# Moving token loads, norms and block splits forward, and spreading transposes and a convolution over steps, in a hybrid mixer layer

## The chip, the cores and the metric

The kernel runs on one core of a Trainium2 chip. The metric is the device time of one execution in microseconds; the number given for a kernel is the median of several runs. One further execution was taken by the hardware profiler, and every row below comes from it.

## The reference, cut to what matters

One layer of a streaming encoder over 512 tokens of width 2048 and 256 memory tokens of the same width:

```python
h = rms_norm(x, norm_g)
proj = h @ w_in                       # 2048 -> 13312
(a_b, a_c, a_x, a_z, q, k, v, b_z, mq, m_z, g_a, g_b, g_m) = split(proj)
ya = (short_conv_mixer(a_b, a_c, a_x, conv_w) * silu(a_z)) @ w_branch_a
yb = (chunk_band_attention(q, k, v, ...) * silu(b_z)) @ w_branch_b
mk, mv = split(rms_norm(mem, mem_norm_g) @ w_mem_kv)
ym = (memory_attention(mq, mk, mv, ...) * silu(m_z)) @ w_branch_m
merged = sigmoid(g_a + b0) * ya + sigmoid(g_b + b1) * yb + sigmoid(g_m + b2) * ym
x = x + merged @ w_out
```

`short_conv_mixer` is `a_b * conv3(a_c * a_x)`, a causal convolution of three taps along the tokens, per channel. So `a_c * a_x` has to be turned (channels on partitions) before the taps, and `a_b * silu(a_z)` likewise before it multiplies the result.

## The kernel before, in words

The program is a list of **steps**. Each step has weight loads, subtractions of weights (`adds`), a split of a weight tile and its matmuls. `run_steps` (line 123) walks the list and emits, for step i, in this order: the loads of step i + 6, the adds of step i, the split of step i + 2, the matmuls of step i, its `post` (the evacuation of finished banks), whatever `at_step(i, ...)` put there, what `after(n, ...)` put there n steps earlier, and then the waiting `task`s as far as a budget of 1.35 per step goes. Every engine runs its own instructions in the order in which they were emitted (class `Engine`, line 40), so this order is the order of each queue. A function that stands later in a step stands behind everything of that step on each engine that it uses.

Steps 0 to 15 are the projection of memory (`kv_steps`, line 405): eight fp32 matmuls of 128x512 each, from a 512 KB weight load `raw_kv` and the turned memory `mT`. Beside them the tokens are made ready: 16 pieces of x of 256 KB are loaded (line 441), one token tile of 128 rows in four pieces; `x_norm(t)` (line 495) takes the squares of the four pieces on ScalarE, the reciprocal root on VectorE and GpSimd, and scales pieces 0 and 2 on VectorE, 1 and 3 on ScalarE; `x_turn(t, k4)` (line 503) turns one piece with four TensorE transposes, and VectorE evacuates it times the gain. `mem_piece` (line 349) does the same for memory.

From step 16 on the projection of the tokens runs in `pair`s of 28 steps (line 235), in the order q, k, v, cx, bz, mqz, az, then the gates. A pair multiplies two halves of the tokens with two column blocks of 512, in the seven-product scheme of Strassen and Winograd: products P1, P5, P6, P3, P7, P2, P4, four steps each. A step has 12 matmuls (two k tiles, two banks, three products of high and low parts). The left operands are the blocks A11, S1, S2, S4, S3, A12, A22 of the normalised tokens, made once: `H.do` (line 477) either combines two blocks with a VectorE operation on 128x1024 per half (s1 to s4), or splits one into a high part (a cast on ScalarE) and a low part (a subtraction on VectorE), also 128x1024 per half. The weights of each step are split in the same way (`split_w`, line 186: `whi` on ScalarE, `wlo` on VectorE; three buffers of each), and 16 of the 28 steps have a weight subtraction before them on VectorE.

Slots of SBUF are shared: S3 takes the slots of the raw memory, A22 high takes the slot of the combination S12, and S2 takes the slots of `mT`, so its low part can be written only after the last matmul of step 15.

The memory projection's results are rescaled by ScalarE (`post` in line 423) at the ends of steps 14 and 15; `heads_out` (line 364) then puts squares, a reciprocal root (`rstd`, over VectorE and GpSimd) and scaling of the keys among the tasks.

In the pair cx, the last product of a half multiplies two evacuated tiles (`go` in line 615) and turns the result (`u_turn`, line 598: four transposes per tile, two copies by ScalarE); both happen at the end of the same step, as tasks. After the last tile `conv` (line 589) runs as one task: for each of four channel groups one ScalarE multiplication and two VectorE operations over 512 tokens. In the pair az, `w_turn` (line 620) does for `a_b * silu(a_z)` what `u_turn` does for `a_c * a_x`.

Of the kernel before, what the change touches and what calls it, by code (L numbers as in the profile page):

```python
# [14 lines left out]
ALU = mybir.AluOpType  # L15
# [5 lines left out]
S = 512  # L21
# [44 lines left out]
def trunk_layer(ctx: ExitStack, tc, x, mem, gx, gm, w_in, w_kv, bg, cw, hg, relz, w_a, w_b, w_m, w_o, out):  # L66
    nc = tc.nc
    PE, ACT, DVE = Engine(tc, nc.tensor), Engine(tc, nc.scalar), Engine(tc, nc.vector)
    POOL, SP = Engine(tc, nc.gpsimd), Engine(tc, nc.sync)
# [17 lines left out]
    cw_sb = cst.tile([P, 3, 4], F32, name="cw_sb")  # L87
# [5 lines left out]
    def slot(i, name, shape=(P, 4, S), dtype=F32):  # L93
        return big.tile(list(shape), dtype, tag=f"s{i}", name=name)

    def cell(name, shape=(P, S)):
        return cel.tile(list(shape), F32, tag="c", name=name)

    def wide(name, shape=(P, 2, S), tag="pp"):
        return hds.tile(list(shape), F32, tag=tag, name=name)  # L100
# [8 lines left out]
    steps, later, todo, at = [], [], [], {}  # L109
# [3 lines left out]
    def after(n, fn):  # L113
        seq[0] += 1
        heapq.heappush(later, (clock[0] + n, seq[0], fn))

    def at_step(i, fn):
        at.setdefault(i, []).append(fn)

    def task(cost, fn):  # L120
        todo.append((cost, fn))
# [213 lines left out]
    def piece(dst, src, t, j):  # L335
        SP.dma_start(dst[:, j, :], src[t * P:(t + 1) * P, j * S:(j + 1) * S])
# [3 lines left out]
    xraw = [slot((13, 12, 3, 2)[t], f"x{t}") for t in range(NT)]  # L340
# [98 lines left out]
        steps[j - 1].loads.append(lambda j=j: first_loads(j))  # L439
    steps[2].loads.append(lambda: [SP.dma_start(d, s) for d, s in ((gx_sb, gx), (hg_sb, hg), (cw_sb, cw))])  # L440
    for i in range(16):
        steps[3 + i // 2].loads.append(lambda i=i: piece(xraw[i // 4], x, i // 4, i % 4))

    for k4 in range(4):
        at_step((-3, 0, 3, 5)[k4], lambda k4=k4: [mem_piece(t, k4) for t in range(NMT)])
# [49 lines left out]
    def x_norm(t):  # L495
        r = row_rstd(squares(xraw[t], f"x{t}"), f"x{t}")
        for j in range(4):
            if j % 2:
                ACT.mul(xraw[t][:, j, :], xraw[t][:, j, :], r)
            else:  # L500
                DVE.tensor_scalar_mul(xraw[t][:, j, :], xraw[t][:, j, :], r)

    def x_turn(t, k4):
        pt = bank(f"pt_x{t}_{k4}", (P, 4, P))
        for j in range(4):
            PE.transpose(pt[:, j, :], xraw[t][:, k4, j * P:(j + 1) * P], ident)
        DVE.tensor_tensor(H.f((k4 // 2, t // 2), k4 % 2)[:, :, (t % 2) * P:(t % 2 + 1) * P], pt,
                          gx_sb[:, 4 * k4:4 * k4 + 4].unsqueeze(2).broadcast_to([P, 4, P]), op=ALU.mult)

    for t in range(NT):  # L510
        b = 2 + 2 * t
        at_step(b, lambda t=t: x_norm(t))
        at_step(b + 1, lambda t=t: [x_turn(t, 0), x_turn(t, 1)])
        at_step(b + 2, lambda t=t: [x_turn(t, 2), x_turn(t, 3)])
    for i in range(2):
        for n, what in ((6 + i, "A11"), (8 + i, "A12"), (11, "s1"), (12, "s3"), (13, "S3"), (14, "S1"), (15, "s2"),
                        (16, "s4"), (17 + i, "S4"), (19 + i, "S2"), (22 + i, "A22")):
            at_step(n, lambda i=i, what=what: H.do(what, i))

    def w_pair(src, c0, c1=None):  # L520
# [15 lines left out]
    y_d = dram.tile([P, 4, S], F32, name="y_d")  # L536
# [18 lines left out]
    def silu(c, name):  # L555
        sg = cell(f"sg_{name}")
        ACT.activation(sg, c, AF.Sigmoid)
        DVE.tensor_mul(c, c, sg)
# [22 lines left out]
    kept, uT = {}, []  # L581

    def turned(c, name, put):
        pt = bank(f"pt_{name}", (P, 4, P))
        for j in range(4):
            PE.transpose(pt[:, j, :], c[:, j * P:(j + 1) * P], ident)
        put(pt)

    def conv():
        for j in range(4):  # L590
            u = uT[j // 2][:, j % 2, :]
            y = cell(f"cv{j}")
            ACT.mul(y, u, cw_sb[:, 2, j:j + 1])
            DVE.scalar_tensor_tensor(y[:, 1:], u[:, :S - 1], cw_sb[:, 1, j:j + 1], y[:, 1:], ALU.mult, ALU.add)
            DVE.scalar_tensor_tensor(y[:, 2:], u[:, :S - 2], cw_sb[:, 0, j:j + 1], y[:, 2:], ALU.mult, ALU.add)
            after(3, lambda j=j, y=y: SP.dma_start(y_d[:, j, :], y))

    def u_turn(t, c):
        if not uT:
            uT.extend(wide(f"uT{i}", tag=("pp", "qk")[i]) for i in range(2))  # L600

        def put(pt):
            for i in range(2):
                ACT.copy(uT[i][:, :, t * P:(t + 1) * P], pt[:, 2 * i:2 * i + 2, :])
        turned(c, f"u{t}", put)
        if t == NT - 1:
            task(1.5, conv)

    def cx_done(half, t0, cells):
        for i, c in enumerate(cells):  # L610
            t = t0 + i
            if half:
                kept["x", t] = c
            else:
                def go(t=t, c=c):
                    DVE.tensor_mul(c, c, kept["x", t])
                    task(0.8, lambda: u_turn(t, c))
                task(0.1, go)

    def w_turn(t, c):  # L620
        def put(pt):
            wt = cell(f"wt{t}", (P, 4, P))
            ACT.copy(wt, pt)
            after(2, lambda: SP.dma_start(wt_d[:, :, t * P:(t + 1) * P], wt))
        turned(c, f"w{t}", put)

    def bz_conv_done(half, t0, cells):
        for i, c in enumerate(cells):
            t = t0 + i
            if half:  # L630
                kept["z", t] = c
                task(0.7, lambda c=c: silu(c, "az"))
            else:
                def go(t=t, c=c):
                    DVE.tensor_mul(c, c, kept["z", t])
                    task(0.8, lambda: w_turn(t, c))
                task(0.1, go)

    pair("cx", H.left, w_pair(w_in, A_C, A_X), cx_done)
# [100 lines left out]
    for u in range(len(units)):  # L740
        i = n_g + EVERY * u
# [174 lines left out]
```

## Time and profile before

| | |
|---|---|
| median of 3 runs | 1528.65 us (1528.4 to 1529.83) |
| the profiled execution | 1527.54 us, its span 1525.8 us, granted TensorE clock 0.997 |
| TensorE busy (matmuls) | 1488.8 us, 98% of the span |
| weight loads of TensorE | 1201.5 us, 79% |
| VectorE busy | 1148.1 us, 75% |
| ScalarE busy | 707.0 us, 46% |
| chain that ended last | TensorE 87%, VectorE 8%, ScalarE 2%, issue 1%, DMA 1% |

The span runs from the first to the last instruction; the profiled time is 1.74 us longer than it. In the rows below PE is TensorE, DVE VectorE, ACT ScalarE, SP the queue that issues loads. In a row of the timeline the columns are start, duration (of the whole group), engine, line, operation, written tile and read tiles, shape, count, and in brackets the idle time before it with what ended it. All instructions carry line 48, a helper's, so tiles tell them apart.

### The profile page before, as it was taken

To read this page: it belongs to the slowest core of one execution; us is meant where nothing else is said; L and a number is where in the kernel's file an instruction comes from. 1 tells how busy PE (TensorE), PEld (TensorE's weight loads), DVE (VectorE), ACT (ScalarE), POOL (GpSimd) and SP (SyncE) were. 2 spreads that over 40 slices of the span, in tenths; PEclk is the share of its full clock that TensorE was granted. 3 is DMA by queue.
4 is the path that set the end of the run, shared out by engine and by line. 5 is a ranking of instruction groups with operands and counts; after the bars stand their busy time and mean duration, and the time that the engine had idled before them with its cause. 6 is when DMAs were issued, how large, how long until landed. Compare 5 with 4: busy or idle time off the path is not lost.

```text
span 1525.8 us, 17874 instructions
## 1 busy us (share of the span) xinstructions
PE 1488.8 (98%) x6696; PEld 1201.5 (79%) x6696; DVE 1148.1 (75%) x1393; ACT 707.0 (46%) x1102; POOL 22.0 (1%) x23
## 2 busy tenths in 40 slices
PE   8989999999899999999999999999999999998998
PEld 4568888788688888788888888888887888886787
DVE  3697778777788887787777878787887455579987
ACT  3665666543444455444444444444445343445442
POOL 0000000000000000000000000000000000000000
PEclk9999999999999999999999999999999999999999
DMA  9524354363426253525537263543736555510724
GB/s 331 180 69 149 126 169 141 99 214 110 138 64 212 65 179 91 186 88 190 169 117 257 90 214 104 176 166 97 254 138 232 193 194 188 204 43 21 248 83 131
DMA packets 139046, 233.45 MB, mean 153 GB/s; under 512 B 9808, under 2 KB 35408, under 8 KB 138320
## 3 DMA queue, kind: packets, MB, share of 16 engines
q1 hardware_dynamic: 130320, 215.54, 43.0%
q10 hardware_dynamic: 8640, 16.78, 3.3%
q8 instruction: 52, 0.85, 0.2%
q14 instruction: 34, 0.28, 0.1%
HBM read 198.73 MB, written 36.17 MB: 154 GB/s over the span
## 4 chain that ended last, share of the span: by engine, by line
PE 87%; DVE 8%; ACT 2%; issue 1%; DMA 1%; POOL 0%; SPq 0%; DVEq 0%; ACTq 0%; POOLq 0%
PE ps_wb L48 6%; PE psY_gb L48 4%; PE psY_ga L48 4%; PE ps_kv L48 3%; PE psY_gm L48 3%; PE psY_o L48 3%; PE psZ_gm L48 3%; PE psZ_gb L48 3%; PE psZ_ga L48 3%; PE ps_wa L48 3%; PE ps_wm L48 3%; PE psY_k L48 2%; PE psY_mqz L48 2%; PE psY_bz L48 2%; PE psY_az L48 2%; PE psY_cx L48 2%
## 5 line engine op out<-in xcount | busy, mean ns | idle before, releaser
L48 ACT CAST whi_o_P<-raw_o 128x1024 fp32r<-128x1024 f32 x56 | 58.7, 1054 | 85.7 <-DVE raw_o L48 21.0
L48 DVE TENSOR_TENSOR wlo_ga_P<-raw_ga,whi_ga_P 128x1024 fp32r<-128x1024 f32 x56 | 68.2, 1222 | 31.9 <-ACT whi_ga_P L48 31.4
L48 DVE TENSOR_TENSOR wlo_gb_P<-raw_gb,whi_gb_P 128x1024 fp32r<-128x1024 f32 x56 | 68.1, 1222 | 31.6 <-ACT whi_gb_P L48 31.5
L48 DVE TENSOR_TENSOR wlo_gm_P<-raw_gm,whi_gm_P 128x1024 fp32r<-128x1024 f32 x56 | 68.4, 1222 | 23.3 <-ACT whi_gm_P L48 23.3
L48 DVE TENSOR_TENSOR wlo_o_P<-raw_o,whi_o_P 128x1024 fp32r<-128x1024 f32 x56 | 68.2, 1221 | 20.1 <-ACT whi_o_P L48 19.9
L48 ACT CAST whi_gm_P<-raw_gm 128x1024 fp32r<-128x1024 f32 x56 | 58.7, 1051 | 20.9 <-PE psV_gm L48 4.8
L48 ACT ACTIVATE p<-p,nm 128x128 f32<-128x128 f32 (+3 forms) x32 | 18.0, 564 | 105.2 <-DVE nm L48 102.2
L48 ACT CAST whi_ga_P<-raw_ga 128x1024 fp32r<-128x1024 f32 x56 | 58.3, 1049 | 9.7 <-PE psY_az L48 3.3
L48 ACT CAST whi_gb_P<-raw_gb 128x1024 fp32r<-128x1024 f32 x56 | 58.4, 1049 | 6.9 <-PE psY_gb L48 2.3
L48 ACT COPY p<-ptp 128x256 f32<-128x256 f32 (+3 forms) x48 | 19.6, 408 | 89.4 <-PE ptp L48 89.4
L48 PE MATMUL ps_kv<-raw_kv,mT 128*128 128x512 f32 x128 | 58.1, 605 | 1.4 <-DMA raw_kv<-in_w_kv 1.4
L48 PE MATMUL ps_wb<-whi_wb,yb_hi 128*128 128x512 f32 x128 | 49.8, 389 | 0.0
L48 PE MATMUL ps_wb<-wlo_wb,yb_hi 128*128 128x512 f32 x128 | 49.8, 389 | 0.0
L48 PE MATMUL ps_wb<-whi_wb,yb_lo 128*128 128x512 f32 x128 | 49.8, 389 | 0.0
L48 ACT CAST whi_cx_P<-raw_cx 128x1024 fp32r<-128x1024 f32 x28 | 29.5, 1055 | 42.4 <-PE psY_cx L48 13.2
L48 DVE TENSOR_TENSOR wlo_cx_P<-raw_cx,whi_cx_P 128x1024 fp32r<-128x1024 f32 x28 | 34.3, 1223 | 18.9 <-ACT whi_cx_P L48 17.2
L48 PEld LDWEIGHTS ps_kv<-raw_kv,mT 128*128 128x128 f32 x128 | 24.2, 195 | 28.4 <-issue 26.4
L48 DVE TENSOR_TENSOR wlo_bz_P<-raw_bz,whi_bz_P 128x1024 fp32r<-128x1024 f32 x28 | 34.2, 1223 | 14.2 <-ACT whi_bz_P L48 14.1
L48 ACT CAST whi_bz_P<-raw_bz 128x1024 fp32r<-128x1024 f32 x28 | 29.5, 1052 | 33.4 <-PE psZ_bz L48 10.0
L48 DVE TENSOR_TENSOR wlo_mqz_P<-raw_mqz,whi_mqz_P 128x1024 fp32r<-128x1024 f32 x28 | 34.2, 1223 | 14.2 <-ACT whi_mqz_P L48 14.2
L48 DVE TENSOR_TENSOR wlo_v_P<-raw_v,whi_v_P 128x1024 fp32r<-128x1024 f32 x28 | 34.1, 1222 | 14.0 <-ACT whi_v_P L48 13.8
L48 ACT CAST whi_mqz_P<-raw_mqz 128x1024 fp32r<-128x1024 f32 x28 | 29.4, 1051 | 31.4 <-PE psZ_mqz L48 10.0
(661 smaller groups left out, 4676.5 us busy)
## 6 DMA issues: line engine op xcount, KB each, us to landing
raw_ga<-in_w_in SPq DMA_DIRECT2D x32, 512.0 KB, 4.7
raw_gb<-in_w_in SPq DMA_DIRECT2D x32, 512.0 KB, 5.2
raw_gm<-in_w_in SPq DMA_DIRECT2D x32, 512.0 KB, 5.2
raw_o<-in_w_o SPq DMA_DIRECT2D x32, 512.0 KB, 6.7
raw_kv<-in_w_kv SPq DMA_DIRECT2D x16, 512.0 KB, 7.7
raw_q<-in_w_in SPq DMA_DIRECT2D x16, 512.0 KB, 4.8
raw_k<-in_w_in SPq DMA_DIRECT2D x16, 512.0 KB, 4.8
raw_v<-in_w_in SPq DMA_DIRECT2D x16, 512.0 KB, 4.5
```

The source lines that it names most:

```text
L48: ins = getattr(self.engine, op)(*args, **kwargs)
```

## The change

The loads of x are attached two steps earlier (steps 1 to 8 in place of 3 to 10). `x_norm` is emitted at steps 1, 3, 4, 6 in place of 2, 4, 6, 8, with its transposes in the two steps after each. The block operations move forward by one to five steps and stand closer: the last, A22, at steps 17 and 18 in place of 22 and 23; s1 and s3 share step 9, s2 and s4 share step 12. `conv` becomes a function of one channel group, called 2, 4, 6 and 8 steps after the last `u_turn`. `u_turn` and `w_turn` are called one step after the multiplication (`after(1, ...)`) and not as tasks of the same step.

```diff
     for i in range(16):
-        steps[3 + i // 2].loads.append(lambda i=i: piece(xraw[i // 4], x, i // 4, i % 4))
+        steps[1 + i // 2].loads.append(lambda i=i: piece(xraw[i // 4], x, i // 4, i % 4))
...
     for t in range(NT):
-        b = 2 + 2 * t
+        b = (1, 3, 4, 6)[t]
         at_step(b, lambda t=t: x_norm(t))
         at_step(b + 1, lambda t=t: [x_turn(t, 0), x_turn(t, 1)])
         at_step(b + 2, lambda t=t: [x_turn(t, 2), x_turn(t, 3)])
     for i in range(2):
-        for n, what in ((6 + i, "A11"), (8 + i, "A12"), (11, "s1"), (12, "s3"), (13, "S3"), (14, "S1"), (15, "s2"),
-                        (16, "s4"), (17 + i, "S4"), (19 + i, "S2"), (22 + i, "A22")):
+        for n, what in ((5 + i, "A11"), (7 + i, "A12"), (9, "s1"), (9, "s3"), (10, "S3"), (11, "S1"), (12, "s2"),
+                        (12, "s4"), (13 + i, "S4"), (15 + i, "S2"), (17 + i, "A22")):
             at_step(n, lambda i=i, what=what: H.do(what, i))
...
-    def conv():
-        for j in range(4):
-            u = uT[j // 2][:, j % 2, :]
-            y = cell(f"cv{j}")
-            ACT.mul(y, u, cw_sb[:, 2, j:j + 1])
...
-            after(3, lambda j=j, y=y: SP.dma_start(y_d[:, j, :], y))
+    def conv(j):
+        u = uT[j // 2][:, j % 2, :]
+        y = cell(f"cv{j}")
+        ACT.mul(y, u, cw_sb[:, 2, j:j + 1])
...
+        after(3, lambda: SP.dma_start(y_d[:, j, :], y))
...
         if t == NT - 1:
-            task(1.5, conv)
+            for j in range(4):
+                after(2 + 2 * j, lambda j=j: conv(j))
...
                     DVE.tensor_mul(c, c, kept["x", t])
-                    task(0.8, lambda: u_turn(t, c))
+                    after(1, lambda: u_turn(t, c))
...
                     DVE.tensor_mul(c, c, kept["z", t])
-                    task(0.8, lambda: w_turn(t, c))
+                    after(1, lambda: w_turn(t, c))
```

## Rows read from the trace of the kernel before

**Rows 1.** Waits of PE, whole span: who waited for whom, us, times, longest.
```profile
PE psX_q L48 <- DVE wlo_q_P L48: 5.7, 2, 4.2
...
PE psX_bz L48 <- DVE wlo_bz_P L48: 2.6, 1, 2.6
PE pt_w L48 <- DVE pg_az L48: 1.6, 1, 1.6
PE pt_u L48 <- DVE pg_cx L48: 1.5, 1, 1.5
PE pt_w L48 <- DVE pa_az L48: 1.5, 1, 1.5
PE pt_u L48 <- DVE pa_cx L48: 1.5, 1, 1.5
PE ps_kv L48 <- DMA raw_kv<-in_w_kv: 1.4, 1, 1.4
PE psY_q L48 <- DVE wlo_q_P L48: 1.2, 1, 1.2
```

**Rows 2.** Stretches: us, busy of PE, PEld, DVE, ACT, POOL; clock, DMA share, GB/s.
```profile
8.00:74.00 66.00, 65.76 (x215) 33.93 (x216) 36.35 (x79) 32.50 (x69) 3.32 (x6) 1.00 0.77 271
418.00:420.00 2.00, 2.00 (x6) 1.52 (x6) 2.00 (x3) 0.00 (x0) 0.00 (x0) 0.50 0.19 67
100.00:105.00 5.00, 5.00 (x24) 4.14 (x23) 5.00 (x5) 4.29 (x5) 0.00 (x0) 1.00 0.37 105
```

**Rows 3.** Timeline of PE about the late splits of q.
```profile
89.45 0.62 PE L48 MATMUL psX_q<-wlo_q_P,hA_hi 128*128 128x512 f32 x1 [4.16 <-DVE wlo_q_P L48]
...
93.66 0.39 PE L48 MATMUL psZ_q<-whi_q_P,hS_hi 128*128 128x512 f32 x1
...
96.39 0.60 PE L48 MATMUL pq_mk<-ident,kv 128*128 128x128 f32 x4
```

**Rows 4.** Timeline of DVE from the end of the memory projection into q.
```profile
72.91 2.36 DVE L48 TENSOR_TENSOR hS_lo<-hf_S,hS_hi 128x1024 fp32r<-128x1024 f32 x2 [1.25 <-ACT hS_hi L48]
...
80.96 1.22 DVE L48 TENSOR_TENSOR wlo_q_P<-raw_q,whi_q_P 128x1024 fp32r<-128x1024 f32 x1
...
84.36 0.16 DVE L48 TENSOR_SCALAR v_mk<-ss_mk 128x8 f32<-128x8 f32 x1
86.35 0.17 DVE L48 TENSOR_TENSOR t_mk<-r_mk 128x8 f32<-128x8 f32 x1 [1.83 <-POOL r_mk L48]
...
87.04 1.22 DVE L48 TENSOR_TENSOR raw_q<-raw_q,raw_q 128x1024 f32<-128x1024 f32 x1
88.17 1.22 DVE L48 TENSOR_TENSOR wlo_q_P<-raw_q,whi_q_P 128x1024 fp32r<-128x1024 f32 x1
```

**Rows 5.** Timeline of ACT in the same stretch.
```profile
71.84 1.98 ACT L48 CAST hS_hi<-hf_S 128x1024 fp32r<-128x1024 f32 x2
73.73 0.31 ACT L48 ACTIVATE junk<-kv 128x128 bf16<-128x128 f32 x1
...
75.34 1.03 ACT L48 CAST whi_q_P<-raw_q 128x1024 fp32r<-128x1024 f32 x1
76.28 1.26 ACT L48 ACTIVATE kv<-ps_kv,rm 128x512 f32<-128x512 f32 x2
```

**Rows 6.** The first tokens: PE's and ACT's timelines, then a stretch (columns as Rows 2).
```profile
14.08 10.46 PE L48 MATMUL ps_kv<-raw_kv,mT 128*128 128x512 f32 x24
...
21.47 0.63 ACT L48 ACTIVATE junk<-x 128x512 bf16<-128x512 f32 x1 [0.63 <-DMA x<-in_x]
...
24.02 1.33 ACT L48 ACTIVATE x<-x,r_x 128x512 f32<-128x512 f32 x2 [1.83 <-DVE r_x L48]
...
12.10:21.40 9.30, 9.30 (x29) 4.47 (x29) 1.29 (x2) 2.17 (x6) 0.00 (x0) 1.00 1.00 345
```

**Rows 7.** One weight load, issued at 11.47 us: KB, us to landing.
```profile
raw_kv<-in_w_kv SPq DMA_DIRECT2D x1, 512.0 KB, 5.2
```

**Rows 8.** Timeline of DVE at the convolution.
```profile
408.78 5.87 DVE L48 SCALAR_TENSOR_TENSOR cv<-uT,cw_sb,cv 128x511 f32<-128x511 f32 x8
```

More of the change, by code (lines that the diff above doesn't have):

```diff
@@ L587, in turned @@
         put(pt)
-    def conv():
-        for j in range(4):
-            u = uT[j // 2][:, j % 2, :]
-            y = cell(f"cv{j}")
-            ACT.mul(y, u, cw_sb[:, 2, j:j + 1])
-            DVE.scalar_tensor_tensor(y[:, 1:], u[:, :S - 1], cw_sb[:, 1, j:j + 1], y[:, 1:], ALU.mult, ALU.add)
-            DVE.scalar_tensor_tensor(y[:, 2:], u[:, :S - 2], cw_sb[:, 0, j:j + 1], y[:, 2:], ALU.mult, ALU.add)
-            after(3, lambda j=j, y=y: SP.dma_start(y_d[:, j, :], y))
+    def conv(j):
+        u = uT[j // 2][:, j % 2, :]
+        y = cell(f"cv{j}")
+        ACT.mul(y, u, cw_sb[:, 2, j:j + 1])
+        DVE.scalar_tensor_tensor(y[:, 1:], u[:, :S - 1], cw_sb[:, 1, j:j + 1], y[:, 1:], ALU.mult, ALU.add)
+        DVE.scalar_tensor_tensor(y[:, 2:], u[:, :S - 2], cw_sb[:, 0, j:j + 1], y[:, 2:], ALU.mult, ALU.add)
+        after(3, lambda: SP.dma_start(y_d[:, j, :], y))
     def u_turn(t, c):
```

## The prediction

> **What bounds the kernel now.** I read the page's shares and chain first: TensorE is busy 98% of the span and is 87% of the chain. So a change pays only where it removes time in which TensorE waits, or runs at half its clock. The second view is the list of TensorE's waits [rows 1]: seven of the lines shown lie in code that the change touches. Two late weight splits in the first pair (psX_q, 5.7 us in two waits, the longest 4.2, so the other 1.5) and a third one there (psY_q, 1.2); one in bz (psX_bz, 2.6); four turns in cx and az (1.5 to 1.6 each). The wait for a weight load of the memory projection (1.4) is at the very start and stays. The third view is the table of stretches [rows 2]: the memory projection from 8 to 74 us has TensorE busy 65.76 of 66 us at clock 1.00, so there is nothing to win there and every wait put in is paid in full. In 418 to 420 us the clock is 0.50, which is the lower of the two levels, 1.2 GHz.
>
> The price of that lower level: after the wait of 4.16 us eleven matmuls take from 89.45 to 93.66, 4.21 us, while the next twelve take 93.66 to 96.39, 2.73 us [rows 3]. Eleven at the full rate would be 2.5, so a long wait costs 1.7 us more than itself. The stretch at 418 us shows the same after the wait of 2.6, and I price it alike.
>
> **The turns.** Today the product of two evacuated tiles and its four transposes are emitted at the end of one step, so TensorE, which has just finished the step's matmuls, waits for two evacuations and two products on VectorE. With the turn one step later, the next step's twelve matmuls, 2.7 us, stand ahead of it, longer than the wait of 1.5 that they cover, and their weights were split two steps before. The transposes and ScalarE's copies are the same work a step later. The four waits go: 1.6 + 1.5 + 1.5 + 1.5 = 6.1 us [rows 1]. What is late next is nothing I can name: the copies now stand behind one more weight cast on ScalarE, which is busy 46% of the span.
>
> **The convolution.** Eight VectorE operations in one run, 5.87 us [rows 8], stand ahead of weight splits that TensorE needs every 2.7 us; that is the wait of 2.6 in bz, with 1.7 of low clock. Spread, one channel group is 5.87 / 4 = 1.47 us every second step. A step of bz has at most a subtraction and a low part, 1.13 us each (from one start to the next [rows 4]), so 2.26 of 2.72 us, leaving 0.46; two such steps and a group are 4.52 + 1.47 = 5.99 against 5.44, an excess of 0.55 per group. Steps 4 and 9 of the pair have no subtraction and give 1.13 back, and P5's evacuation of two halves adds about one operation, 1.13, at step 7. The worst backlog, at step 8, is near 2 to 2.5 us. Splits are emitted two steps ahead, which left 5.87 - 2.6 = 3.3 us of delay free today. So it fits: 2.6 + 1.7 = 4.3 us go. Bounds: all 4.3, or 2.6 if a wait of an excess too small for a clock drop is left.
>
> **The start of q.** Here the sum is made queue by queue. On ScalarE, from the end of the first rescale at 71.84 [rows 5]: a cast takes (73.73 - 71.84) / 2 = 0.95, four squares 75.34 - 73.73 = 1.61, a weight cast 0.94, the second rescale about 1.15. Today's order is two casts of S1, four squares, weight cast of step 17, rescale. After the change: one cast of S4 (72.8), four squares (74.4), weight cast of step 17 (75.3), rescale (76.5), cast of S2 (77.4), two squares (78.2), weight cast of step 18 (79.2), cast of S2 (80.1), two squares (80.9). On VectorE the eight operations of s2, s4 and S1 that now fall here (two of them waited 1.25 for a cast at 72.91 [rows 4]) are gone to steps 11 and 12, where VectorE has room: it is busy 36.35 of 66 us there [rows 2]. In their place S2's low parts come in: first half after its cast, 77.5; subtraction 78.6; low part of step 18 from 79.8 to 81.0, where it ends at 82.18 today; second half of S2, then the keys' reciprocal root at 82.05. That takes 87.04 - 84.36 = 2.68 us, of which 1.83 is waiting for GpSimd [rows 4]. So subtraction at 84.7, low part of step 19 from 85.9 to 87.1, where today it ends at 89.4. TensorE waits 0.4 us before step 18 and 3.3 before step 19, in place of 1.5 and 4.16, and the clock falls again: 2.3 us won. This assumes that the moved S4 and S3 are done by 74; steps 9 to 15 take 7 x 3.44 = 24 us, so the last tokens are evacuated by about 52; two roots of memory at 2.68 at most and fourteen operations at 1.13 are 21 us, so 73. After step 19 VectorE has only A22's two low parts in place of six of S4, S2 and A22, so that the full queue of today (5.00 of 5.00 us at 100 to 105 [rows 2]) drains and the 1.2 us of psY_q go. Bounds for the start of q: 0 won, if what is now late is as late as today, to 5.7 + 1.2 + 1.7 = 8.6, all of it.
>
> That the reciprocal root holds up a subtraction whose operands are long there is seen in the 1.83 us of idle VectorE at 86.35 [rows 4]; without it the low part of step 19 would end 1.8 us earlier, and the gain at q would be 4.1 in place of 2.3. The Trainium skill states the rule (TensorE: Matmul & The Clock Gate, section on the array as 16 sub-arrays): ScalarE and VectorE are strict FIFO, nothing passes a waiting instruction. It speaks against this change, since S2 now waits in step 15 for a cast that stands behind the rescale. By that rule, and the trace agrees, the sum keeps 2.3.
>
> **The loads and norms of x.** The fourth piece of x lands just before 21.47 [rows 6]. It goes ahead of the two weight loads of 512 KB that stand before it now, 1.05 MB at 345 GB/s [rows 6], so 3.0 us earlier, 18.4. From landing to scaling took 24.02 - 21.47 = 2.55 us, and the first scaled piece 0.5 to 0.7 more: 21.5 to 21.7. TensorE's three steps from 14.08 to 24.4 [rows 6] are 3.44 each, so it reaches the first transposes, now after step 2, at 20.95. It waits 0.7 us, paid in full; nothing else is queued there but the next step's matmuls. The bounds: 0, and 3.7 if the piece gains nothing on its landing today. The later sets have more lead: the eighth piece comes 2.1 MB or 6.1 us later, 24.5, is scaled by 27.7, and its transposes come up after step 4, past 28. On SP the weight load of step 3, issued at 11.47 and landed 5.2 us later [rows 7], has 1 MB of x put before it: 19.7, needed at 21.7 or later. VectorE's evacuation of two transposes stands behind the second norm to about 29.5; four banks are free for transposes, and two of them are evacuated before. GpSimd only does the roots.
>
> **The sum.** 6.1 + 4.3 + 2.3 + 1.2 - 0.7 = 13.2 us. The profiled execution takes 1527.5, its span 1525.8; less 13.2 it is 1514.3. The median of the runs is 1.1 above the profiled one, so I predict 1515.4.
>
> **Rivals.** (a) *The start of q is cured altogether*: 8.6 in place of 3.5 there, 1510.3. For it: twelve VectorE operations leave that stretch. Against it: ScalarE's order above. (b) *Nothing is won at q*: S2 waits for the last memory matmul and holds both queues as long as today's operations do, or x is late by as much as q wins. Only turns and convolution remain: 1528.65 - 10.4 = 1518.3, or 1522.0 with the worst wait for x. (c) *The turn's and convolution's waits only move*: ScalarE's copies and VectorE's groups delay the next weight splits by as much. Then 13.2 - 10.4 = 2.8 us are won, 1525.9, no change. Against it: splits have 3.3 us of free delay. That would be the change not doing what it says. (d) *Slower*: x starves TensorE. Each of the four norms comes late, TensorE stands at its transposes 2.7 us each time and each time falls to half clock: 4 x (2.7 + 1.7) = 17.6, against 13.9 won elsewhere, 3.7 above now, 1532.3. It decides where the four waits with their low clock pass 13.9, 3.5 each. For it: DMA runs at 345 GB/s with all engines busy from 12 to 21 us. Against it: x moves ahead by no more than 1 MB of weights. The Trainium skill (DMA: Bandwidth & Descriptors, section on issuing engines) says that all transfers run on the same 16 DMA engines and interleave, so x and the weights do share. By that rule weights land later; no run here shows yet whether TensorE would feel it.
>
> **How the numbers follow.** Chances: the forecast 0.57, (a) 0.12, (b) 0.17, (c) 0.08, (d) 0.06. About 0.2%, 3 us, is what a measurement of this kernel can tell from no change. Forecast, (a) and (b) are faster, with a small part of (d)'s milder forms: 0.87. (c) is the same, with some of (d): 0.07. Slower: 0.06. The range runs from a little under (a), 1509.5, to the worst of (b), 1522.
>
> **What would show it.** Right: the four lines pt_u and pt_w and the line psX_bz gone from TensorE's waits; psX_q still there with 3 to 4 us, no psY_q; one wait for x of under 1 us near 21; clock 1.00 at 418 us and still a drop after step 18. Wrong: new waits for pt_x of 2 us or more, TensorE waiting for weight splits in the steps after a turn, or q begun without a wait.

## The result, and the profile after

| | before | after |
|---|---|---|
| median of 4 runs each | 1528.53 us (1526.74 to 1529.83) | 1516.63 us (1515.63 to 1517.05) |
| ratio after to before | | 0.9926, 95% interval 0.9914 to 0.9937 |
| the profiled execution | 1527.54 us, span 1525.8 | 1515.63 us, span 1513.8 |
| TensorE busy, granted clock | 1488.8 us, 0.997 | 1486.6 us, 0.999 |

The change wins 11.9 us where 13.2 were forecast; by the interval of the ratio it is 9.6 to 13.1. TensorE's waits of the kernel after, over the whole span, who waited for whom, us, times, longest; the lines that answer to [rows 1], and the new ones:

```profile
PE psX_q L48 <- DVE wlo_q_P L48: 4.4, 3, 3.1
...
PE pt_x L48 <- DVE mT L48: 0.7, 1, 0.7
PE pt_x L48 <- DVE x L48: 0.6, 1, 0.6
...
PE psX_q L48 <- ACT whi_q_P L48: 0.5, 1, 0.5
PE ps_kv L48 <- DMA raw_kv<-in_w_kv: 0.3, 1, 0.3
...
PE psZ_ga L48 <- DVE wlo_ga_P L48: 0.2, 1, 0.2
```

The two lines pt_u, the two pt_w, psX_bz and psY_q are gone. psX_q has shrunk from 5.7 to 4.4 + 0.5, and two waits of the token transposes are new. Stretches of the kernel after, columns as in [rows 2]:

```profile
8.00:74.00 66.00, 64.58 (x211) 32.67 (x210) 41.79 (x84) 31.76 (x66) 3.32 (x6) 1.00 0.79 271
76.00:95.00 19.00, 14.06 (x51) 10.08 (x50) 14.32 (x17) 14.89 (x33) 1.65 (x1) 0.91 0.35 111
88.00:94.00 6.00, 3.07 (x8) 2.45 (x9) 5.90 (x9) 3.02 (x6) 0.00 (x0) 0.72 0.00 0
383.00:416.00 33.00, 33.00 (x156) 27.50 (x155) 27.29 (x29) 16.36 (x24) 0.00 (x0) 1.00 0.40 126
418.00:420.00 2.00, 2.00 (x10) 1.67 (x9) 2.00 (x3) 1.55 (x2) 0.00 (x0) 1.00 0.36 131
```

From 383 to 416 us, over the turns of cx and the beginning of bz, TensorE has no gap left, and at 418 us the clock is 1.00 where it was 0.50 [rows 2]. From 8 to 74 us TensorE, which had been full (65.76 of 66), now has 64.58. And at the start of q the clock still falls (0.72 between 88 and 94 us).

Waits alone don't say where time was won. For that I compare when the same product begins in two profiled executions; each number of the table is the start in a run less that in the profiled execution before, in us. A difference between two columns is what the stretch between them won or lost.

| run | q begins | its second product | its fourth | cx begins | bz begins | late in bz | in the gate ga | last pair |
|---|---|---|---|---|---|---|---|---|
| the change | +2.00 | +1.20 | -0.24 | -0.13 | -4.75 | -8.44 | -11.90 | -11.9 |
| turns alone | +0.12 | +0.12 | +0.13 | +0.15 | -4.46 | -1.02 | -4.49 | -4.5 |
| turns and convolution | +0.64 | +0.47 | +0.52 | +0.62 | -3.99 | -7.69 | -11.15 | -11.2 |
| loads, norms, blocks alone | +1.73 | +1.06 | -0.39 | -0.32 | -0.35 | -0.33 | -0.36 | -0.4 |
| convolution alone | +1.27 | +1.93 | +1.97 | +1.99 | +1.97 | -1.56 | -1.54 | -1.5 |

The change's row reads from left to right: 2.0 us lost in the memory projection, 0.8 won in the first product of q, 1.4 in the next two, nothing in k and v, then 11.8 in cx, bz, az and ga. Of these 11.8 the turns hold 7.3 and the convolution 4.5. When bz begins in the new kernel, the last turn of cx has not run yet; it now stands behind bz's first step. A turn takes 0.79 us (the one before it runs from 391.94 to 392.73 us), so cx won 4.62 - 0.79 = 3.8, and bz, which now holds that turn, won 8.44 - 4.75 + 0.79 = 4.5; az and what follows won 3.5. The convolution now stands on VectorE in four pairs of 1.53 us, the first at 410.08 and the last at 428.84 in its timeline below, where it was one run of 5.87 [rows 8]. TensorE's timeline shows the first turn of cx, in the kernel before and then in the kernel after (columns as in [rows 3]):

```profile
391.04 1.26 PE L48 MATMUL pt_u<-ident,pg_cx 128*128 128x128 f32 x8 [1.53 <-DVE pg_cx L48]
...
391.94 1.03 PE L48 MATMUL pt_u<-ident,pg_cx 128*128 128x128 f32 x8
```

**Where the memory projection lost 2.0.** TensorE's timeline of the kernel after, first in the memory projection, then in q (columns as in [rows 3]):

```profile
21.62 1.06 PE L48 MATMUL pt_x<-ident,x 128*128 128x128 f32 x8 [0.60 <-DVE x L48]
22.52 3.60 PE L48 MATMUL ps_kv<-raw_kv,mT 128*128 128x512 f32 x8
...
31.41 1.06 PE L48 MATMUL pt_x<-ident,x 128*128 128x128 f32 x8
...
38.34 1.32 PE L48 MATMUL pt_x<-ident,x 128*128 128x128 f32 x8 [0.68 <-DVE mT L48]
...
84.85 0.50 PE L48 MATMUL psX_q<-wlo_q_P,hA_hi 128*128 128x512 f32 x1 [0.76 <-DVE wlo_q_P L48]
...
90.93 0.79 PE L48 MATMUL psX_q<-wlo_q_P,hA_hi 128*128 128x512 f32 x1 [3.07 <-DVE wlo_q_P L48]
91.52 0.63 PE L48 MATMUL psX_q<-whi_q_P,hA_lo 128*128 128x512 f32 x1
...
94.86 0.40 PE L48 MATMUL psZ_q<-whi_q_P,hS_hi 128*128 128x512 f32 x1
```

The wait of 0.60 at 21.62 is the one forecast; the step that holds it is 0.8 longer than its work. Two more steps are late. The transposes at 31.41 come 0.3 after the matmuls ahead of them would have let them begin. The step that ends at 39.49 has 1.1 too much: the wait of 0.68, and a turn of 1.32 in place of 1.06. (A small gap of 0.16 that the kernel before had at 53 us is gone.) VectorE's timeline of the kernel after shows why, and serves the next readings too (columns as in [rows 4]):

```profile
27.80 1.28 DVE L48 TENSOR_TENSOR hf<-pt_x,gx_sb 128x512 f32<-128x512 f32 x2
29.00 0.15 DVE L48 TENSOR_REDUCE ss_x<-ss_x 128x1 f32<-128x4 f32 x1
...
35.02 0.16 DVE L48 TENSOR_REDUCE ss_x<-ss_x 128x1 f32<-128x4 f32 x1 [1.65 <-ACT junk L48]
...
36.80 0.88 DVE L48 TENSOR_SCALAR x<-x,r_x 128x512 f32<-128x512 f32 x2
37.60 1.28 DVE L48 TENSOR_TENSOR mT<-pt_mem,gm_sb 128x512 f32<-128x512 f32 x2
...
68.61 1.22 DVE L48 TENSOR_TENSOR hf_S<-hf,hf_S 128x1024 f32<-128x1024 f32 x1
...
71.00 1.23 DVE L48 TENSOR_TENSOR hf_S<-hf,hf_S 128x1024 f32<-128x1024 f32 x1
...
85.84 0.17 DVE L48 TENSOR_SCALAR v_mk<-ss_mk 128x8 f32<-128x8 f32 x1
87.83 0.17 DVE L48 TENSOR_TENSOR t_mk<-r_mk 128x8 f32<-128x8 f32 x1 [1.82 <-POOL r_mk L48]
...
88.53 1.22 DVE L48 TENSOR_TENSOR raw_q<-raw_q,raw_q 128x1024 f32<-128x1024 f32 x1
89.66 1.22 DVE L48 TENSOR_TENSOR wlo_q_P<-raw_q,whi_q_P 128x1024 fp32r<-128x1024 f32 x1
...
410.08 1.53 DVE L48 SCALAR_TENSOR_TENSOR cv<-uT,cw_sb,cv 128x511 f32<-128x511 f32 x2
...
428.84 1.53 DVE L48 SCALAR_TENSOR_TENSOR cv<-uT,cw_sb,cv 128x511 f32<-128x511 f32 x2
```

The second norm's root starts at 29.00 with no idle time before it: it stands behind that step's four evacuations (two of memory, two of x), emitted ahead of it, although its squares were done at 25.9. The scaling of its tokens began at 30.78. The third case is the reverse: the evacuation of `mT` at 37.60 is behind the third norm, which waited 1.65 us for squares at 35.02 and then for GpSimd. TensorE needs the bank that this evacuation frees. The new order put norms and turns of neighbouring tokens into the same steps, and each queue keeps the order in which they were emitted.

**Why q won so little.** ScalarE's timeline of the kernel after (columns as in [rows 5]):

```profile
72.26 1.04 ACT L48 CAST hS_hi<-hf_S 128x1024 fp32r<-128x1024 f32 x1 [8.04 <-DVE hf_S L48]
73.21 1.04 ACT L48 CAST whi_q_P<-raw_q 128x1024 fp32r<-128x1024 f32 x1
74.16 1.26 ACT L48 ACTIVATE kv<-ps_kv,rm 128x512 f32<-128x512 f32 x2
75.31 1.04 ACT L48 CAST hS_hi<-hf_S 128x1024 fp32r<-128x1024 f32 x1
76.24 0.31 ACT L48 ACTIVATE junk<-kv 128x128 bf16<-128x128 f32 x1
...
78.80 1.25 ACT L48 ACTIVATE kv<-ps_kv,rm 128x512 f32<-128x512 f32 x2
79.95 1.04 ACT L48 CAST hS_hi<-hf_S 128x1024 fp32r<-128x1024 f32 x1
...
84.39 1.04 ACT L48 CAST whi_q_P<-raw_q 128x1024 fp32r<-128x1024 f32 x1
```

The first cast of S4 waited 8.04 us for s4, whose second half VectorE did only at 71.00 to 72.2. (The cast reads the first half alone, which was done at 69.8, yet it began only after the second.) A weight cast and the keys' first rescale stand behind that cast, so the rescale ended at 75.31. That is 3.5 later than the 71.84 of the kernel before [rows 5], 2.0 of it from the memory projection and 1.5 from the cast. All that follows on ScalarE is late by these 1.5: the second rescale ended at 79.95 where the forecast, with the shift of 2.0, would have 78.5. On VectorE the keys' root comes at 85.84 and again idles 1.82 us for GpSimd; the low part that TensorE wants comes at 89.66; TensorE waits 3.07 at 90.93 and its matmuls then last 0.63 in place of 0.39.

### The profile page after: what moved, and what is told of

Its sections match the earlier page's. It is cut to its first block, busy times and chain, and to the rows that moved or that the text cites. A ratio compares the mean times of both kernels' runs of the same rounds, so it can differ in the third digit from the quotient of the medians.

```text
span 1513.8 us, 17882 instructions
## 1 busy us (share of the span) xinstructions
PE 1486.6 (98%) x6696; PEld 1201.1 (79%) x6696; DVE 1148.2 (76%) x1393; ACT 706.7 (47%) x1102; POOL 22.0 (1%) x23
## 4 chain that ended last, share of the span: by engine, by line
PE 85%; DVE 9%; ACT 2%; issue 1%; DMA 1%; POOL 1%; SPq 0%; DVEq 0%; POOLq 0%; ACTq 0%
PE ps_wb L48 6%; PE psY_gb L48 4%; PE psY_ga L48 4%; PE psY_gm L48 3%; PE psY_o L48 3%; PE psZ_gm L48 3%; PE psZ_gb L48 3%; PE ps_wa L48 3%; PE ps_wm L48 3%; PE psZ_ga L48 3%; PE psY_k L48 2%; PE psY_cx L48 2%; PE psY_mqz L48 2%; PE psY_bz L48 2%; PE psY_q L48 2%; PE psY_az L48 2%
## 5 line engine op out<-in xcount | busy, mean ns | idle before, releaser
L48 ACT CAST whi_cx_P<-raw_cx 128x1024 fp32r<-128x1024 f32 x28 | 29.6, 1056 | 42.9 <-PE psY_cx L48 13.2
L48 DVE TENSOR_TENSOR wlo_q_P<-raw_q,whi_q_P 128x1024 fp32r<-128x1024 f32 x28 | 34.2, 1223 | 12.5 <-ACT whi_q_P L48 12.3
```

Of the source, the lines that this page charges most:

```text
L48: ins = getattr(self.engine, op)(*args, **kwargs)
```

## The experiments

The first five experiments cut the change into parts; the others try the two explanations above and what follows from them. A time after the word "before" is the median of the kernel before on the same chip.

**1. Turns alone** (on the kernel before):

```diff
-                    task(0.8, lambda: u_turn(t, c))
+                    after(1, lambda: u_turn(t, c))
...
-                    task(0.8, lambda: w_turn(t, c))
+                    after(1, lambda: w_turn(t, c))
```

> The kernel before with the two turns alone moved one step later. Theory (each wait belongs to its own part): the four waits pt_u and pt_w are gone, the wait psX_bz stays; the pair of traces showed 2.7 us won from the end of cx's first half to its next product, and 3.5 us over az into the first gate, so about 6.5 us in all, 1522. Rival (the waits only move, to the splits behind ScalarE's copies): new waits for weight splits in the steps after a turn of 1 us and more each, and under 3 us won, 1526 or more.

Measured: 1522.17 us (1521.59 to 1523.57; before 1527.72), ratio 0.9963, interval 0.995 to 0.9976. The turns' waits are gone, but the wait in bz has grown. In the waits of this kernel:

```profile
PE psX_bz L48 <- DVE wlo_bz_P L48: 4.0, 1, 4.0
```

It was 2.6 [rows 1]. The clock between 414 and 420 us is 0.51, against 0.78 in the kernel before. The convolution, still one run of 5.88 us on VectorE, now begins 5.2 us after bz's first product (406.48 against 401.28) where it began 3.0 after it (408.78 against 405.74): it waits for the turn that was put off, and so ends later against TensorE's steps. The turns win 7.3 us here too (3.8 in cx, 3.5 in az, by the table), and 2.7 are lost again in bz (4.46 - 1.02, less the turn of 0.79).

**2. Turns and convolution, without the front part** (on the kernel after, loads, norms and blocks put back):

```diff
-        steps[1 + i // 2].loads.append(lambda i=i: piece(xraw[i // 4], x, i // 4, i % 4))
+        steps[3 + i // 2].loads.append(lambda i=i: piece(xraw[i // 4], x, i // 4, i % 4))
...
-        b = (1, 3, 4, 6)[t]
+        b = 2 + 2 * t
...
-        for n, what in ((5 + i, "A11"), (7 + i, "A12"), (9, "s1"), (9, "s3"), (10, "S3"), (11, "S1"), (12, "s2"),
-                        (12, "s4"), (13 + i, "S4"), (15 + i, "S2"), (17 + i, "A22")):
+        for n, what in ((6 + i, "A11"), (8 + i, "A12"), (11, "s1"), (12, "s3"), (13, "S3"), (14, "S1"), (15, "s2"),
+                        (16, "s4"), (17 + i, "S4"), (19 + i, "S2"), (22 + i, "A22")):
```

> The changed kernel with loads, norms and blocks put back to where they stood before, so that turns and convolution parts alone are changed. Theory: all that was won after the first pair stays, 8.3 us in cx and bz and 3.4 us in az and the first gate, 11.7 us in all, 1517; the start of q is that of the kernel before to 0.1 us. The rival by the prediction's own terms (turns and convolution 10.4, the front 2.8) gives 1518.1 here.

Measured: 1516.85 us (1516.12 to 1517.47; before 1527.72), ratio 0.9927, interval 0.9913 to 0.9942. This is the ratio of the whole change (0.9926). So the gain is all in the turns and the convolution, and the front part, on which 2.8 us of the forecast rested, gives nothing that can be measured.

**3. Loads, norms and blocks alone** (on the kernel before; the diff of experiment 2 with its signs changed):

> The kernel before with loads, norms and blocks of x alone moved. Theory: the first product of q starts 2.0 us later than before and the third product group psZ_q 0.2 us earlier, so 0.25 us are won, no change that a measurement can tell, 1528.3; after 120 us the trace is that of before. Rival (the prediction's term): 2.8 us won, 1525.7.

Measured: 1526.7 us (1525.63 to 1528.35, 10 runs; before 1527.72), ratio 0.9992, interval 0.9982 to 1.0001. The table has +1.73 at the start of q and -0.36 at the end, and the waits are those of the change:

```profile
PE psX_q L48 <- DVE wlo_q_P L48: 4.4, 3, 3.1
...
PE pt_x L48 <- DVE mT L48: 0.7, 1, 0.7
PE psX_q L48 <- ACT whi_q_P L48: 0.6, 1, 0.6
```

The front part loses in the projection about what it wins in q. By the medians it wins 1.0 us, with an interval from 2.7 won to 0.2 lost, so no gain is shown.

**4. The loads alone two steps earlier** (on the kernel before):

```diff
-        steps[3 + i // 2].loads.append(lambda i=i: piece(xraw[i // 4], x, i // 4, i % 4))
+        steps[1 + i // 2].loads.append(lambda i=i: piece(xraw[i // 4], x, i // 4, i % 4))
```

> The kernel before with the loads of x alone two steps earlier, norms, transposes and blocks where they were. Theory (the memory projection's new waits come from where norms and transposes stand, not from the transfers): q's first product starts at 74.1 us as before, no wait for a weight load of memory beyond the 0.3 to 1.4 us at its first step, time that of the kernel before within 1 us. Rival (x takes bandwidth from the memory projection's weights): q starts 1 us later or more, with waits of ps_kv for raw_kv.

Measured, in one run: 1527.57 us (before 1527.72). q begins 0.02 us later than in the kernel before, and the wait for a memory weight is 1.0 where it was 1.4 [rows 1]. In this run putting x ahead of weights costs nothing, which speaks against the transfers of rival (d): the 2.0 us of the projection come from where the norms and turns stand, with the first wait (0.60) being one for the tokens themselves.

**5. The convolution alone spread** (on the kernel before; the call):

```diff
-            task(1.5, conv)
+            for j in range(4):
+                after(2 + 2 * j, lambda j=j: conv(j))
```

> The kernel before with the convolution alone spread, turns as before. Turns alone won 4.5 us by the trace and made the wait of bz 4.0 us in place of 2.6; turns and convolution together won 11.1. Theory (the convolution's wait is one of its own and the turns shift it): convolution alone wins its 2.6 and 1.7, 4.3 us, 1523.4, and the remaining 2.3 us of the pair belong to neither alone. Rival (spreading pays the whole difference, 6.7): 1521.

Measured: 1524.87 us (1523.84 to 1526.82, 10 runs; before 1528.09), ratio 0.9978, interval 0.9968 to 0.9988. By the table it wins 3.5 us (+1.97 at bz, -1.56 late in it), less than the 4.5 that it wins beside the turns, since its own trace has a new wait. TensorE's timeline of this kernel:

```profile
436.05 0.50 PE L48 MATMUL psY_bz<-wlo_bz_P,hS_hi 128*128 128x512 f32 x1 [0.64 <-DVE wlo_bz_P L48]
```

The last group stands on VectorE at 432.19, ahead of the low part that is wanted here. With the turns put off, every group falls one step later, and no such wait is seen. So by the traces neither part has its full worth without the other: 4.6 and 3.5 alone, 11.8 together. The medians point the same way (5.6 and 3.2 alone, 10.9 in experiment 2), but their intervals are too wide to show it; the new waits in the rows do. That the step of the group makes the difference is read from the traces and was not tried by itself.

**6. Later blocks** (on the kernel after): are the splits of S2 and A22 in ScalarE's and VectorE's queues what delays the low part of step 19?

```diff
-                        (12, "s4"), (13 + i, "S4"), (15 + i, "S2"), (17 + i, "A22")):
+                        (12, "s4"), (13 + i, "S4"), (20 + 2 * i, "S2"), (27 + 2 * i, "A22")):
```

> The changed kernel with S2 split at steps 20 and 22 and A22 at 27 and 29, in place of 15 and 16, 17 and 18. Theory A (the start of q is held up by the splits of S2 and A22 that now stand there: four casts of 0.95 us on ScalarE and four low parts of 1.13 us on VectorE): the low part of step 19 is ready about 2.3 us earlier, the 4.9 us of waits of psX_q fall to about 2.5, the clock may still fall, 2 to 4 us won against the changed kernel. Theory B (it is the keys' squares on ScalarE, eight of 0.43 us, and the reciprocal root on VectorE, 2.7 us): under 1.5 us won.

Measured, in one run: 1513.57 us (before 1527.83). psX_q's waits are 3.1 in three, the longest 1.9, and q's second product begins 2.2 us earlier than after the change; 2.1 of it are kept to the end. So these two blocks are a part of it; the edit moved both, and does not tell them apart. The root is still there: VectorE idles 1.82 us for it in this run too.

**7. The keys' norm put off eleven steps** (on the kernel after):

```diff
-                            heads_out("mk", cells, 0, hg_sb[:, 3:4], lambda t: mk_d[:, :, t * P:(t + 1) * P])
+                            after(11, lambda: heads_out("mk", cells, 0, hg_sb[:, 3:4],
+                                                        lambda t: mk_d[:, :, t * P:(t + 1) * P]))
```

> The changed kernel with the keys' norm (squares, reciprocal root, scaling, turns) put off by eleven steps, from step 14 to step 25, everything else the same. Theory B (keys' squares and root hold up the start of q): the longest wait of psX_q, 3.1 us before the low part of step 19, goes, and with it the fall of the clock, 4 to 6 us won against the changed kernel. Theory A (S2 and A22): less than 2.5 us won, waits of 2.5 us and more stay.

Measured, in one run: 1515.49 us (before 1527.83). q's second product begins 6.0 us earlier than after the change, and in the stretch of q the clock stays at 1.00:

```profile
76.00:95.00 19.00, 17.23 (x72) 12.73 (x71) 18.09 (x16) 13.17 (x16) 0.00 (x0) 1.00 0.35 111
```

But 4.6 of it are left when v begins, 0.2 when cx does, and 0.14 at the end: most is given back in v. VectorE's timeline of this kernel there:

```profile
278.47 0.69 DVE L48 TENSOR_TENSOR pe_v<-psY_v,pa_v 128x512 f32<-128x512 f32 x1 [4.60 <-PE pq_k L48]
```

An evacuation of v had to wait 4.60 us for the transposes of k's tiles (0.20 in the kernel before). The reason as I read it: the waiting tasks are one list with a budget, and the keys' tasks, eleven steps later, push those of q and k back, until the kernel's nine cells (its buffers for evacuated tiles) are all held. TensorE then waits 2.8 us (psZ_v). Experiment 10 tests this reading.

**8. Order within the memory projection** (on the kernel after): memory's last groups are turned at steps 1 and 2, each token is turned before the next norm is emitted.

```diff
-        at_step((-3, 0, 3, 5)[k4], lambda k4=k4: [mem_piece(t, k4) for t in range(NMT)])
+        at_step((-3, 0, 1, 2)[k4], lambda k4=k4: [mem_piece(t, k4) for t in range(NMT)])
...
-        b = (1, 3, 4, 6)[t]
-        at_step(b, lambda t=t: x_norm(t))
-        at_step(b + 1, lambda t=t: [x_turn(t, 0), x_turn(t, 1)])
-        at_step(b + 2, lambda t=t: [x_turn(t, 2), x_turn(t, 3)])
+        b = (2, 4, 5, 7)[t]
+        at_step(b, lambda t=t: [x_turn(t, 0), x_turn(t, 1)])
+        at_step(b + 1, lambda t=t: [x_turn(t, 2), x_turn(t, 3)])
+    for t in range(NT):
+        at_step((1, 2, 3, 5)[t], lambda t=t: x_norm(t))
```

> The changed kernel with memory's third and fourth groups turned at steps 1 and 2 in place of 3 and 5, and with the norms of x put at steps 1, 2, 3, 5 ahead of the evacuations that they stood behind. Theory (the 2.0 us by which q starts late are TensorE waiting for x's first set, 0.7, for the second set's norm that stands behind four evacuations, 0.3, and for banks whose evacuations stand behind the third norm, 0.9 to 1.1): q's first product starts at 74.1 to 74.5 us in place of 76.1, and about 1 to 2 us are won in all, as the start of q moves forward with it. Rival (the transfers are late): q still starts at 75.5 us or later.

Measured, in one run: 1513.35 us (before 1527.83). Neither pt_x line is in the waits; from the second step of the projection to q there are 59.9 us (14.72 to 74.58) where the change has 62.1 (13.99 to 76.09), and 2.3 us are kept to the end. This run reached that second step 0.7 us later than the change, which alone could have hidden the wait for the first tokens. Experiment 11 has the same order, reaches the step at 13.73, and still takes 59.85 us to q with no wait for x. So the loss in the projection was one of order, as read above.

**9. Experiments 6, 7 and 8 together** (their three edits):

> The changed kernel with all three: blocks S2 and A22 later, keys' norm put off, memory's turns and x's norms reordered. Theory: the memory projection ends at 74.1 to 74.5 us, psX_q waits under 1 us in all, no fall of the clock at q; against the changed kernel 2.0 us in the projection and 4.9 + 1.7 us at the start of q, less 0.5 left over, 7 to 8 us won, 1509. Rival (ScalarE's and VectorE's order at the start of q sets another wait as long, from sums of weights and splits alone): under 4 us won, 1513 or more.

Measured: 1512.66 us (1512.28 to 1512.99; before 1527.83), ratio 0.9899, interval 0.9883 to 0.9916. A miss: q's second product is 8.9 us earlier than after the change, and the same wait in v (2.8) comes back, so that 2.7 are left.

**10. The keys' norm put off nine steps, alone** (on the kernel after):

```diff
-                            heads_out("mk", cells, 0, hg_sb[:, 3:4], lambda t: mk_d[:, :, t * P:(t + 1) * P])
+                            after(9, lambda: heads_out("mk", cells, 0, hg_sb[:, 3:4],
+                                                        lambda t: mk_d[:, :, t * P:(t + 1) * P]))
```

> The changed kernel with the keys' norm put off by nine steps and nothing else. Theory (task list, as above): 5 to 6 us won at q's second product group as with eleven steps, 3 to 5 of them kept after v, 1512. Rival (cells run out in v whatever the delay): under 1 us kept, 1515.5.

Measured, in one run: 1511.96 us (before 1528.09). q's second product begins 5.3 us earlier than after the change, 3.7 are kept to the end, and v has no wait over 0.3. In the waits of this kernel and in the stretch of q:

```profile
PE psX_q L48 <- DVE wlo_q_P L48: 1.0, 2, 0.7
```

```profile
76.00:95.00 19.00, 17.28 (x70) 12.50 (x69) 17.63 (x17) 13.80 (x16) 0.00 (x0) 1.00 0.35 111
```

Two steps less, and the evacuation of v waits 0.20 for k's transposes as in the kernel before. That bears out the reading of experiment 7. More cells, the direct test of it, were not tried, so that the cells are the cause is argued, not shown.

**11. Experiments 6 and 8 with the norm put off nine steps** (in experiment 9's kernel):

```diff
-                            after(11, lambda: heads_out("mk", cells, 0, hg_sb[:, 3:4],
+                            after(9, lambda: heads_out("mk", cells, 0, hg_sb[:, 3:4],
```

> The changed kernel with later S2 and A22, memory's turns and x's norms reordered, and the keys' norm put off by nine steps in place of eleven. Theory (what the delay by eleven lost again in v, 4.3 us, came from the task list: the keys' tasks ended two steps after q's began at step 31, so all later tasks of q and k were two steps late and the cells ran out in v; by nine they end at step 30): the start of q keeps most of its 8.9 us, no wait of 2.8 us in v, against the changed kernel 6 to 7.5 us won, 1509.5. Rival (the loss in v belongs to the earlier start itself, the loads or the cells not keeping up): the trace falls back in v as with eleven, 2.7 us won, 1513.

Measured: 1506.03 us (1505.12 to 1506.07; before 1528.09), ratio 0.9855, interval 0.984 to 0.987. It beats both kernels. TensorE is full from the memory projection into q, as these stretches of this kernel show:

```profile
8.00:74.00 66.00, 66.00 (x217) 33.93 (x216) 43.78 (x86) 34.42 (x70) 3.32 (x6) 1.00 0.78 270
76.00:95.00 19.00, 19.00 (x85) 15.71 (x85) 17.49 (x17) 11.70 (x16) 0.00 (x0) 1.00 0.34 111
```

## Why the prediction was right, and where its terms were off

The forecast was 1515.4 us, and 1516.63 came. The time is that of the likeliest case, and the mechanism of turns and convolution is right. The front part went otherwise than forecast: it was priced 2.7 too high, and turns and convolution 1.4 too low.

- **The turns**: forecast 6.1, measured 7.3. The mechanism was as stated: the next step's matmuls cover the wait, and but for 0.2 us in ga no weight split of the following steps is late, so rival (c) is out for the change as a whole (for the turns alone a part of it was true, experiment 1). The term was too small for two reasons. The first is that the rows of waits count from the modelled end of a matmul. Such a matmul is listed with 0.39 us while the next one starts 0.23 later. The Trainium skill says so (Perfetto Trace Analysis, section on the tensor engine's instruction): the profiler estimates TensorE's end times. The trace agrees, since successive rows overlap. In bz before, for example, the row has 2.55 while one start to the next is 2.94, 2.71 more than the usual step. Counted from start to start the four waits are 6.7 us. The second reason is that TensorE was slower just after each wait: from its start to the next matmul a turn took 1.0 us in the kernel before and takes 0.79 now, 0.9 less in all four, and the step behind each was 0.05 slower. That makes 7.8, of which the wait in ga takes back 0.5.
- **The convolution**: forecast 4.3, measured 4.5, the wait of 2.7 and 1.7 of low clock. Right, with the condition that experiments 1 and 5 add: the turns must be put off too.
- **Loads and norms of x**: forecast a loss of 0.7, measured 2.0. The wait for the first tokens was right (0.60 in its row, 0.8 with the pace). The step that failed is the claim that later sets have more lead: the second set was to be scaled by 27.7, and its scaling began at 30.78. I followed when x lands, and of VectorE's queue wrote down only one evacuation behind the second norm. In the trace the second norm itself stands behind evacuations, and another evacuation behind the third norm. Experiment 4 clears the loads, experiment 8 gets 2.2 back by order alone.
- **The start of q**: forecast 2.3, measured 0.8. The step that failed is "This assumes that the moved S4 and S3 are done by 74", which I checked by summing VectorE's work (73), and not by who waits for its last piece. s4 ended at 72.2, but S4's first cast waited for it on ScalarE, ahead of the first rescale: 1.5 us late beyond the shift of 2.0, and S4's second low part ended only at 77.6. I had also counted two squares behind S2's cast where four stand (cast and squares last from 79.95 to 82.50), some 0.9 more on ScalarE, of which VectorE's queue hid all but 0.3: the root came at 85.84 where the forecast with the shift of 2.0 had 84.05. So the low part of step 19 was 1.8 later than forecast, against which the fall of the clock cost 0.3 less (3.93 in place of 4.21 for eleven matmuls); together that is the 1.5 between 2.3 and 0.8. The prediction's two waits there, 0.4 and 3.3, do not fit its own times: they would be 2.0 won, and the low part at 87.1 in place of 89.4 makes the second wait 3.0. The trace has 4.9 of psX_q in all, more than the 3 to 4 given as a sign of being right. That the keys' root holds up the subtraction (1.83 forecast, 1.82 seen) was right. The rule of the Trainium skill that the prediction weighed (TensorE: Matmul & The Clock Gate, section on the array as 16 sub-arrays), strict FIFO on ScalarE and VectorE, agrees with the trace: the rescale passed no waiting cast. I had applied it to S2 and not to S4.
- **The wait of psY_q**: forecast 1.2, measured 1.4 with the pace. Right.
- **Rivals.** For the front part (b) is what happened: x was late by about as much as q won, 0.1 won in all by the table where (b) said 0 and the forecast 2.8. But (b) came to 1518.3 to 1522, since it too priced turns and convolution at 10.4 in place of 11.8. So that 1516.63 lies nearer to the forecast than to (b) is luck: two errors of opposite sign met, 2.7 and 1.4, which leaves the 1.3 us between 13.2 and 11.9. (a) needed the keys' root out of the way, as experiment 10 shows.

## What to carry to other kernels

Work that is moved earlier is not free because the engine has room in that stretch: write the queues of all engines out in order, and look for a waiting instruction that now stands ahead of something TensorE needs. Small serial chains (a reciprocal root over two engines) cost little by themselves and much where they stand; putting one off by nine steps won 3.7 us in one run, where the whole front part of the change won 0.1. Two edits that share a stretch should be timed alone and together, since here 4.6 and 3.5 made 11.8 by the traces; and where tasks share a budget and a pool of buffers, a delay that wins at its place can come back as a wait for a buffer far behind it.

## What the hardware showed that I had not expected

- The price of a fall of the clock is not one number. The eleven matmuls between the long wait and q's second product take 2.5 us at the full rate. They took 4.21 after a wait of 4.16 in the kernel before [rows 3], 3.93 after 3.07 in the kernel after (90.93 to 94.86), 4.21 after only 1.94 in experiment 6, and 4.87 after the same wait of 4.2 in experiment 5, whose code there is that of the kernel before. So it was 1.4 to 2.4 us where I had taken 1.7, and it did not follow the length of the wait.
- With the code up to q unchanged, q began 0.12, 0.64 and 1.27 us later than in the profiled execution before (experiments 1, 2 and 5). The traces show where: all of it is there when the second step of the memory projection begins (14.20, 14.72 and 15.35 against 14.08). Why is open: the first step's eight matmuls are listed with 5.13 us in the kernel before and 6.63 in experiment 5 (first and second line below). They start 0.85 us apart for longer there, against 0.43 from the second step on, while the granted clock from 7 to 13 us is 1.00 in both. So single profiled times of this kernel differ by over 1 us without a cause in the code, and I trust the differences between two marks of a trace more than its end.

```profile
8.24 5.13 PE L48 MATMUL ps_kv<-raw_kv,mT 128*128 128x512 f32 x8 [1.36 <-DMA raw_kv<-in_w_kv]
...
8.01 6.63 PE L48 MATMUL ps_kv<-raw_kv,mT 128*128 128x512 f32 x8 [1.14 <-DMA raw_kv<-in_w_kv]
```
